# Softmax reciprocals as powers on GpSimd, and the scaling of one attention's probabilities on ScalarE

## The chip, the core and the metric

The kernel runs on one core of one Trainium2 chip. The metric is the device time of one execution in microseconds (us). TensorE (PE in the profile; its weight loads are PEld) multiplies matrices, VectorE (DVE) and ScalarE (ACT) work on columns of up to 128 partitions, GpSimd (POOL) does small work beside them, and SyncE (SP) issues most loads. Each engine runs its own instructions in a fixed order; between engines an instruction waits for semaphores that others raise.

## The reference

A two-layer decoder trunk on 512 tokens of width 1024, in float32. What matters here are its two attentions, both causal, with 8 heads:

```python
# layer 0, differential attention: two softmaxes per head, d = 64
s = einsum('bqhcd,bkhcd->bhcqk', q_blk, k) * d ** -0.5
p = softmax(where(causal, s, -inf))
a = p[:, :, 0] - lam * p[:, :, 1]
o = einsum('bhqk,bkhe->bqhe', a, v)        # then RMSNorm over each head
# layer 1, latent attention: shared keys and values, one softmax per head
s = (einsum(qn, k_nope) + einsum(qr, k_rope)) * (128 + 64) ** -0.5
p = softmax(where(causal, s, -inf))
o = einsum('bhqk,bkhe->bqhe', p, v)
```

Around them stand RMSNorms, the projections, rotary embeddings and a squared-ReLU MLP of width 4096 in each layer.

## The kernel before

**Matrices.** Each float32 operand is split into a high and a low part (`...h`, `...l`) and each product is three matmuls (`mm3`, lines 359 to 361), so TensorE has work nearly all the time. The splits cost VectorE and ScalarE time: ScalarE copies the high part of a weight (line 108), VectorE subtracts it for the low part (line 120).

**The two attention stages.** A task is one head (8) and one block of 128 query rows (4), so there are 32 tasks in the differential attention (`task_a`, names a00 to a73: head, block) and 32 in the latent attention (`task_b`, b00 to b73). Block i looks at n = 128 (i + 1) keys. The tasks are Python generators. A `Weave` steps through the active tasks, and between steps it pulls matmuls of the next heads' projections (`Filler`), so that the tasks' waits lie beside other matmuls. `LAG_A` and `LAG_B` say how many steps a task lets pass before each of its parts. A scheduler then sets the order in which each engine's instructions stand, by what each of them waits for; no order in these stages is written out by hand.

**One task of the differential attention.** TensorE writes two score tiles into PSUM (tile `s`, two banks). VectorE adds the mask and takes the smallest of the negated row (line 531, a pair of instructions for each softmax). ScalarE takes the exponential, with the row sums as a second result (line 533): z0 and z1. Then VectorE works out one column, f = z0 · nlam / z1, in two instructions (lines 585 and 586), and adds p1 · f to p0 (line 587; z0 goes out in the later RMSNorm). In `attend` TensorE transposes the block (tile `tr`, two banks, line 334), ScalarE and VectorE copy its high and low parts (`ath`, `atl`, lines 553 and 554), and after every second block TensorE multiplies with the values (tile `o`, one bank).

**One task of the latent attention.** One score tile, the same mask and exponential with the row sum `tot`, then VectorE takes 1/tot (line 622) and multiplies the whole block by it (line 623), and `attend` follows. The head's result is split from the bank `o` (`onh` on ScalarE, `onl` on VectorE, lines 345 and 346) before the next head may write there.

**GpSimd** has little to do: sums of squares (line 376), powers of -0.5 for the RMSNorms (lines 330 and 606, and at the end `fr`), a scaling near the end.

`small` gives one-column tiles out of a ring of 48. Lines with number 51 in the profile belong to the stretches at the start and the end whose order is kept as the program has it.

Of the kernel before, what the change touches and what calls it, by code (L numbers as in the profile page):

```python
# [10 lines left out]
F32 = mybir.dt.float32  # L11
F32R = mybir.dt.float32r
AF = mybir.ActivationFunctionType
ALU = mybir.AluOpType

P = 128
# [257 lines left out]
def trunk(ctx: ExitStack, tc: tile.TileContext, io: dict, out: bass.AP):  # L274
    nc = Engines(tc)
    PSUM = bass.MemoryType.PSUM

    const = ctx.enter_context(tc.tile_pool(name="const", bufs=1))
# [7 lines left out]
    def big(name, dt=F32):  # L286
        return ap.tile([P, T], dt, name=name, tag="big", bufs=NBIG)

    def small(name, n=8):
        return ap.tile([P, n], F32, name=name, tag="small", bufs=48)  # L290

    def bank(name, tag):
        return ps.tile([P, T], F32, name=name, tag=tag, bufs=BANKS[tag])
# [38 lines left out]
    def transposes(dst, src_of, n=NT):  # L332
        for i in range(n):
            nc.tensor.transpose(dst[:, i * P:(i + 1) * P], src_of(i), ident)

    def row_ps(cols, name):

        dst = bank(name + "_ps", "tr")
        transposes(dst, lambda i: cols[:, i:i + 1].to_broadcast([P, P]))
        return dst  # L340
# [10 lines left out]
    def split(src, name, scale=None, tiles=None):  # L351
        h, l = tiles or (big(name + "h", F32R), big(name + "l", F32R))
        split_into(h, l, src, scale)
        return h, l

    def mm3(dst, a, b, start, stop, **kw):

        (ah, al), (bh, bl) = a, b
        nc.tensor.matmul(dst, ah, bh, start=start, stop=False, **kw)  # L359
        nc.tensor.matmul(dst, ah, bl, start=False, stop=False, **kw)  # L360
        nc.tensor.matmul(dst, al, bh, start=False, stop=stop, **kw)  # L361
        us = 3 * PASS * max(256, dst.shape[-1])
        later.spent(us)
        return us

    def sub(pair, *idx):
        return tuple(t[idx] for t in pair)
# [122 lines left out]
    def mm2(dst, q, k, rest, tok, n, start):  # L490

        nc.tensor.matmul(dst, q[:, tok], k[:, :n], start=start, stop=False)
        nc.tensor.matmul(dst, q[:, tok], rest[:, :n], start=False, stop=True)
        later.spent(2 * PASS * max(256, n))
# [27 lines left out]
    def wait(ticks):  # L522
        for _ in range(ticks):
            yield

    def softmax_parts(s, i, scale, total, name):

        n = P * (i + 1)
        st = small(name + "st", 1)
        sm = big(name + "sm")  # L530
        nc.vector.tensor_tensor_reduce(
            sm[:, :n], s[:, :n], mask[:, T - n:], -scale, 3e38, ALU.add, ALU.min, st)
        nc.scalar.activation(sm[:, :n], sm[:, :n], AF.Exp, bias=st, scale=-1.0, accum_out=total)
        return sm
# [8 lines left out]
    def attend(hd, a, i, lag):  # L543

        name, gq, ii = hd.name, i // 2, i % 2
        if ii == 0:
            hd.a = [ap.tile([P, 4, 2 * P], F32R, name=f"{name}at{n}{gq}", tag=f"at{n}", bufs=2) for n in "hl"]
        ath, atl = hd.a
        tr = bank(f"{name}tr{i}", "tr")
        transposes(tr, lambda j: a[:, j * P:(j + 1) * P], i + 1)  # L550
        cols = (ALL, slice(0, i + 1), slice(ii * P, (ii + 1) * P))
        src = tr[:, :(i + 1) * P].rearrange("p (j q) -> p j q", q=P)
        nc.scalar.copy(ath[cols], src)
        nc.vector.tensor_sub(atl[cols], src, ath[cols].bitcast(F32))
        if ii == 0:
            return
        yield from wait(lag)
        if gq == 0:
            hd.o = bank(name + "o", "o")
        weave.need(lambda: len(hd.quarter.v) == 2)  # L560
        vs = hd.quarter.vs(hd.hh)
        for j in range(i + 1):
            lo = P if j == i else 0
            mm3(hd.o[:, gq * 2 * P + lo:(gq + 1) * 2 * P], vs(j), (ath[:, j, lo:], atl[:, j, lo:]), j == 0, j == i)

    def task_a(hd, i, heads):

        name, n, tok = hd.name, P * (i + 1), slice(i * P, (i + 1) * P)
        qt = hd.quarter
        weave.need(lambda: len(qt.qs) > hd.hh and len(qt.ks) > hd.hh)  # L570
        q, k = qt.qs[hd.hh], qt.ks[hd.hh]
        if i == 0:
            hd.z = small(name + "z", 4)
        z0, z1 = hd.z[:, i:i + 1], small(name + "z1", 1)
        got = []
        for c in range(2):
            s = bank(f"{name}s{i}{c}", "s")
            mm2(s[:, :n], q[c], k[0][c], k[1][c], tok, n, True)
            got.append(softmax_parts(s, i, SCALE_A, (z0, z1)[c], f"{name}{i}{c}"))
        if i == NT - 1:  # L580
            keys_read.add(hd.at)
        yield from wait(LAG_A[1])
        p0, p1 = got
        f = small(name + "f", 1)
        nc.vector.reciprocal(f, z1)
        nc.vector.tensor_scalar(f, f, z0, nlam, op0=ALU.mult, op1=ALU.mult)
        nc.vector.scalar_tensor_tensor(p0[:, :n], p1[:, :n], f, p0[:, :n], op0=ALU.mult, op1=ALU.add)
        yield from wait(LAG_A[2])
        yield from attend(hd, p0, i, LAG_A[3])
        if i < NT - 1:  # L590
            return
        yield from wait(LAG_N[0])
        osb = big(name + "osb")
        nc.scalar.copy(osb, hd.o)
        yield from wait(LAG_N[1])
        otok = bank(name + "otok", "tr")
        transposes(otok, lambda j: osb[:, j * P:(j + 1) * P])
        ss, r = small(name + "ss", 4), small(name + "r", 4)
        junk = big(name + "junk")
        for j in range(NT):  # L600
            cols = slice(j * P, (j + 1) * P)
            nc.scalar.activation(junk[:, cols], otok[:, cols], AF.Square, accum_out=ss[:, j:j + 1])
        e = small(name + "e", 4)
        nc.vector.scalar_tensor_tensor(e, hd.z, SUBLN_EPS, hd.z, op0=ALU.mult, op1=ALU.mult)
        nc.vector.scalar_tensor_tensor(e, ss, 1.0 / P, e, op0=ALU.mult, op1=ALU.add)
        nc.gpsimd.tensor_tensor(r, e, mhalf.to_broadcast([P, 4]), op=ALU.pow)
        yield from wait(LAG_N[2] + LAG_N[3])
        rbo = row_ps(r, name + "rb")
        nc.vector.scalar_tensor_tensor(osb, osb, gsub, rbo, op0=ALU.mult, op1=ALU.mult)
        heads[hd.at] = split(osb, name + "on")  # L610

    def task_b(hd, i, heads):
        name, n, tok = hd.name, P * (i + 1), slice(i * P, (i + 1) * P)
        qt = hd.quarter
        weave.need(lambda: len(qt.qs) > hd.hh and len(qt.ks) > hd.hh and qt.qr and krs)
        s = bank(f"{name}s{i}", "s")
        mm3(s[:, :n], sub(qt.qs[hd.hh], ALL, tok), sub(qt.ks[hd.hh], ALL, slice(0, n)), True, False)
        mm2(s[:, :n], qt.qr[0][hd.hh], *krs[0], tok, n, False)
        tot, rcp = small(name + "tot", 1), small(name + "rc", 1)
        p = softmax_parts(s, i, SCALE_B, tot, f"{name}{i}")  # L620
        yield from wait(LAG_B[1])
        nc.vector.reciprocal(rcp, tot)
        nc.vector.tensor_scalar_mul(p[:, :n], p[:, :n], rcp)
        yield from wait(LAG_B[2])
        yield from attend(hd, p, i, LAG_B[3])
        if i == NT - 1:
            yield from wait(LAG_N[0])
            heads[hd.at] = split(hd.o, name + "on")
# [496 lines left out]
    def late_loads():  # L1125
        nc.sync.dma_start(mask, io["c_mask"])
        for n, name in enumerate(("lambda_q1", "lambda_k1", "lambda_q2", "lambda_k2")):
            nc.sync.dma_start(lam4[:, n, :], io[name].broadcast_to([P, HD]))
    mhalf = const.tile([P, 1], F32, name="mhalf")
    nc.kept = True  # L1130
    nc.vector.memset(mhalf, -0.5)
    ones = const.tile([P, P], F32R, name="ones")
    nc.vector.memset(ones.bitcast(F32), 1.0)
    many = big("many", F32R)
# [74 lines left out]
    for i in range(NT):  # L1209
# [10 lines left out]
    nlam = const.tile([P, 1], F32, name="nlam")  # L1220
# [10 lines left out]


    tasks = [task_a(hd, i, heads_a) for hd in (Head(f"a{h}", h, quarters_a[h // 2], h % 2) for h in range(NH))
             for i in range(NT)]
    fill = Filler(fill_a)
# [71 lines left out]
    def stages(gen, *at):  # L1307
        for us in at:
# [5 lines left out]
    Filler([dq, dkv, krj] + first_b).drain()  # L1314

    tasks = [task_b(hd, i, heads_b) for hd in (Head(f"b{h}", h, quarters_b[h // 2], h % 2) for h in range(NH))
             for i in range(NT)]
    fill = Filler(fill_b)
# [76 lines left out]
```

## Time and profile before

| | us |
|---|---|
| median of 3 runs | 1123.54 (1123.17 to 1124.42) |
| the profiled execution | 1124.63 |
| its span in the trace | 1122.9 |

Of the span TensorE is busy 1106.7 us (99%), VectorE 805.2 (72%), ScalarE 588.8 (52%), GpSimd 61.6 (5%). The differential attention runs from about 50 to 240 us, the latent attention from about 652 to 740 us. A busy share is an average over stages: within the two attentions VectorE is far busier than 72%, which a table of stretches shows. A row of a timeline has its start, its length, the engine, the line, the operation and the tiles (result<-operands); in brackets stands the idle time ahead of it and what ended it.

### The profile page before, as it was taken

What the parts mean: (1) busy time and instruction counts of PE and PEld (TensorE: products, weight loads), DVE (VectorE), ACT (ScalarE), POOL (GpSimd) and SP (SyncE); (2) the same over time, 40 slices, a digit from 0 to 9 for tenths busy, and PEclk for the clock granted to TensorE, in tenths of its full rate; (3) what the DMA queues carried; (4) which work ended last, traced back from release to release, by engine and by line L of the source; (5) the groups of instructions that cost most, each with busy time, mean ns of one, the idle gap of its engine ahead of it and who ended that gap; (6) DMA issues with size and microseconds to landing.
All of it is one profiled execution on the core that took longest, in us unless ns stands there. A gap on an engine that the chain in (4) does not pass through costs nothing. (4 is left out here: it accounts for less than half of the span.)

```text
span 1122.9 us, 14485 instructions
## 1 busy us (share of the span) xinstructions
PE 1106.7 (99%) x5434; PEld 925.3 (82%) x5434; DVE 805.2 (72%) x1417; ACT 588.8 (52%) x1114; POOL 61.6 (5%) x56
## 2 busy tenths in 40 slices
PE   8999999999999999999999999999999999999997
PEld 7889998878888888888887889888888888888885
DVE  6998989964765875886675898855296686687533
ACT  6566666654555455454344666535545445445333
POOL 1000000031000000000022000003000000000011
PEclk8999999999999999999999999999999999999999
DMA  7321221245242142111332211133414315311221
GB/s 230 107 75 57 76 76 58 67 143 155 66 147 97 57 150 94 57 57 40 111 94 90 80 57 38 57 131 94 150 39 150 113 38 161 103 38 57 76 76 75
DMA packets 92517, 102.09 MB, mean 91 GB/s; under 512 B 5104, under 2 KB 74398, under 8 KB 92446
## 3 DMA queue, kind: packets, MB, share of 16 engines
q1 hardware_dynamic: 91166, 99.51, 28.2%
q10 hardware_dynamic: 1280, 1.65, 0.4%
q8 instruction: 43, 0.70, 0.3%
q14 instruction: 28, 0.23, 0.1%
HBM read 99.05 MB, written 2.10 MB: 90 GB/s over the span
## 5 line engine op out<-in xcount | busy, mean ns | idle before, releaser
L359 PE MATMUL m1u<-xn0h,m1u_0h 128*128 128x512 f32 x128 | 50.4, 393 | 0.0
L359 PE MATMUL m1u<-xn1h,m1u_1h 128*128 128x512 f32 x128 | 50.2, 392 | 0.0
L361 PE MATMUL m1u<-xn0h,m1u_0l 128*128 128x512 f32 x128 | 50.0, 390 | 0.0
L360 PE MATMUL m1u<-xn0l,m1u_0h 128*128 128x512 f32 x128 | 50.0, 390 | 0.0
L359 PE MATMUL m0u<-xm0h,m0u_0h 128*128 128x512 f32 x128 | 50.0, 390 | 0.0
L361 PE MATMUL m0u<-xm0h,m0u_0l 128*128 128x512 f32 x128 | 50.0, 390 | 0.0
L361 PE MATMUL m1u<-xn1h,m1u_1l 128*128 128x512 f32 x128 | 49.9, 390 | 0.0
L360 PE MATMUL m1u<-xn1l,m1u_1h 128*128 128x512 f32 x128 | 49.9, 390 | 0.0
L360 PE MATMUL m0u<-xm0l,m0u_0h 128*128 128x512 f32 x128 | 49.9, 390 | 0.0
L361 PE MATMUL m0u<-xm1h,m0u_1l 128*128 128x512 f32 x128 | 49.9, 390 | 0.0
L360 PE MATMUL m0u<-xm1l,m0u_1h 128*128 128x512 f32 x128 | 49.9, 390 | 0.0
L359 PE MATMUL m0u<-xm1h,m0u_1h 128*128 128x512 f32 x128 | 49.8, 389 | 0.0
L120 DVE TENSOR_TENSOR m1u_1l<-m1u_1r,m1u_1h 128x1024 fp32r<-128x1024 f32 x16 | 19.6, 1226 | 32.4 <-ACT m1u_1h L108 32.0
L120 DVE TENSOR_TENSOR m0u_1l<-m0u_1r,m0u_1h 128x1024 fp32r<-128x1024 f32 x16 | 19.9, 1246 | 28.0 <-ACT m0u_1h L108 27.7
L108 ACT CAST m1u_1h<-m1u_1r 128x1024 fp32r<-128x1024 f32 x16 | 16.8, 1052 | 42.5 <-PE m1u L360 29.3
L120 DVE TENSOR_TENSOR m0u_0l<-m0u_0r,m0u_0h 128x1024 fp32r<-128x1024 f32 x16 | 19.9, 1245 | 25.7 <-ACT m0u_0h L108 25.6
L120 DVE TENSOR_TENSOR m1u_0l<-m1u_0r,m1u_0h 128x1024 fp32r<-128x1024 f32 x16 | 19.6, 1224 | 26.0 <-ACT m1u_0h L108 26.0
L108 ACT CAST m0u_1h<-m0u_1r 128x1024 fp32r<-128x1024 f32 x16 | 16.8, 1051 | 40.5 <-PE m0u L360 29.7
L345 ACT CAST krest<-m0A 128x512 fp32r<-128x512 f32 x36 | 22.0, 618 | 27.1 <-PE m0w L360 13.7
L345 ACT CAST krest<-m1A 128x512 fp32r<-128x512 f32 x36 | 22.0, 618 | 26.4 <-PE m1w L360 14.6
L346 DVE TENSOR_TENSOR krest<-m0A,krest 128x512 fp32r<-128x512 f32 x36 | 24.5, 687 | 15.1 <-ACT krest L345 15.1
L346 DVE TENSOR_TENSOR krest<-m1A,krest 128x512 fp32r<-128x512 f32 x36 | 24.4, 687 | 14.0 <-ACT krest L345 14.0
(2905 smaller groups left out, 3719.9 us busy)
## 6 DMA issues: line engine op xcount, KB each, us to landing
m0u_0r<-in_w_up SPq DMA_DIRECT2D x16, 512.0 KB, 3.8
m0u_1r<-in_w_up SPq DMA_DIRECT2D x16, 512.0 KB, 3.7
m1u_0r<-in_w_up SPq DMA_DIRECT2D x16, 512.0 KB, 3.7
m1u_1r<-in_w_up SPq DMA_DIRECT2D x16, 512.0 KB, 4.3
m0B<-in_w_down SPq DMA_DIRECT2D x12, 512.0 KB, 4.3
m0B<-in_w_down SPq DMA_DIRECT2D x24, 256.0 KB, 5.2
m1B<-in_w_down SPq DMA_DIRECT2D x12, 512.0 KB, 3.7
res<-in_w_down SPq DMA_DIRECT2D x12, 512.0 KB, 3.6
```

The source lines that it names most:

```text
L108: self.nc.scalar.copy(d(h), v(self.raws[n]))
L120: eng.tensor_sub(d(to), v(self.raws[n]), d(h).bitcast(F32))
L345: nc.scalar.copy(h, src)
L346: nc.vector.tensor_sub(l, src, h.bitcast(F32))
L359: nc.tensor.matmul(dst, ah, bh, start=start, stop=False, **kw)
L360: nc.tensor.matmul(dst, ah, bl, start=False, stop=False, **kw)
L361: nc.tensor.matmul(dst, al, bh, start=False, stop=stop, **kw)
```

## The change

It touches the reciprocals of both attentions:

```diff
@@ task_a
+        rz1 = small(name + "rz", 1)
+        nc.gpsimd.tensor_tensor(rz1, z1, mone, op=ALU.pow)
         yield from wait(LAG_A[1])
         p0, p1 = got
         f = small(name + "f", 1)
-        nc.vector.reciprocal(f, z1)
-        nc.vector.tensor_scalar(f, f, z0, nlam, op0=ALU.mult, op1=ALU.mult)
+        nc.vector.scalar_tensor_tensor(f, z0, nlam, rz1, op0=ALU.mult, op1=ALU.mult)
         nc.vector.scalar_tensor_tensor(p0[:, :n], p1[:, :n], f, p0[:, :n], op0=ALU.mult, op1=ALU.add)
@@ task_b
         p = softmax_parts(s, i, SCALE_B, tot, f"{name}{i}")
+        nc.gpsimd.tensor_tensor(rcp, tot, mone, op=ALU.pow)
         yield from wait(LAG_B[1])
-        nc.vector.reciprocal(rcp, tot)
-        nc.vector.tensor_scalar_mul(p[:, :n], p[:, :n], rcp)
+        nc.scalar.activation(p[:, :n], p[:, :n], AF.Copy, scale=rcp)
@@ constants
+    mone = const.tile([P, 1], F32, name="mone")
+    nc.vector.memset(mone, -1.0)
```

GpSimd gets 64 powers of one column, each issued right behind its exponentials. VectorE loses a reciprocal in each of the 64 tasks and the scaling in 32; ScalarE gets the 32 scalings. The scheduler also moves other instructions. On TensorE the order of the differential attention stays as it was up to a place in head a7, and in the latent attention some groups of scores and transposes stand a few rows later.

On VectorE, in the differential attention, head a7, block 0 (`a700sm` and `a701sm` are the two probability tiles, `res<-oa` adds an output projection to the residual), the kernel before has

```order
L531 ISA a701sm,a701st<-a7s_2544,mask 128x128
L531 ISA a701st 128x1
L447 TENSOR_TENSOR res<-oa_2552,res 128x512
L585 RECIPROCAL a7f<-a7z_2536 128x1
L586 TENSOR_SCALAR a7f<-a7f,a7z,nlam 128x1
L587 SCALAR_TENSOR_TENSOR a700sm<-a701sm,a7f,a700sm 128x128
```

and the changed kernel, at the same place,

```order
L531 ISA a701sm,a701st<-a7s_2574,mask 128x128
L531 ISA a701st 128x1
L587 SCALAR_TENSOR_TENSOR a7f<-a7z,nlam,a7rz 128x1
L447 TENSOR_TENSOR res<-oa_2584,res 128x512
L588 SCALAR_TENSOR_TENSOR a700sm<-a701sm,a7f,a700sm 128x128
```

Two columns have become one, which now stands right behind the mask of its own softmax, with the addition to the residual behind it.

On ScalarE, in the latent attention's last head and a half (`b5onh` is the high part of head b5's result, `b6ath` and `b7ath` copies of transposed blocks, `b7rc` the reciprocals), the kernel before has

```order
L533 ACTIVATE b71sm,b7tot<-b71sm,b71st 128x256
L345 CAST b5onh<-b5o 128x512
L553 CAST b6ath_7175<-b6tr_7197 128x4x128
L533 ACTIVATE b72sm,b7tot<-b72sm,b72st 128x384
L553 CAST b7ath_7229<-b7tr_7231 128x128
L533 ACTIVATE b73sm,b7tot<-b73sm,b73st 128x512
```

and the changed kernel has

```order
L533 ACTIVATE b70sm,b7tot<-b70sm,b70st 128x128
L624 ACTIVATE b70sm<-b70sm,b7rc 128x128
L553 CAST b6ath_7210<-b6tr_7212 128x3x128
L533 ACTIVATE b71sm,b7tot<-b71sm,b71st 128x256
L345 CAST b5onh<-b5o 128x512
L624 ACTIVATE b71sm<-b71sm,b7rc 128x256
L533 ACTIVATE b72sm,b7tot<-b72sm,b72st 128x384
L553 CAST b6ath_7210<-b6tr_7232 128x4x128
L624 ACTIVATE b72sm<-b72sm,b7rc 128x384
L533 ACTIVATE b73sm,b7tot<-b73sm,b73st 128x512
L553 CAST b7ath_7264<-b7tr_7266 128x128
L624 ACTIVATE b73sm<-b73sm,b7rc 128x512
```

A scaling (line 624) follows each exponential, in the case of b70 with nothing between the two; over the 32 tasks there are eleven such pairs.

## Rows read from the trace of the kernel before

**Rows 1.** Busy time by stretch; columns as the first line says.
```profile
core 0: us, PE busy (x) PEld busy (x) DVE busy (x) ACT busy (x) POOL busy (x), PEclk, DMA share, GB/s
50.00:100.00 50.00, 49.31 (x263) 41.52 (x262) 48.53 (x118) 32.45 (x73) 0.00 (x0) 1.00 0.24 74
100.00:150.00 50.00, 49.62 (x343) 45.73 (x342) 44.36 (x119) 35.65 (x94) 3.40 (x3) 1.00 0.22 65
150.00:222.00 72.00, 71.80 (x437) 62.73 (x435) 66.20 (x173) 48.09 (x130) 3.41 (x3) 1.00 0.21 66
652.00:722.00 70.00, 69.69 (x445) 62.07 (x444) 61.41 (x176) 42.91 (x111) 0.00 (x0) 1.00 0.17 54
```
**Rows 2.** PE's waits in both attentions: us in total, times, longest.
```profile
PE a1tr L334 <- DVE a120sm L587: 0.4, 1, 0.4
PE a1o L360 <- DVE a1atl L554: 0.3, 1, 0.3
...
PE b1o L359 <- DVE b0onl L346: 0.3, 1, 0.3
```
**Rows 3.** What VectorE waited for ahead of line 585: first and last of ten.
```profile
  ACT a521sm L533: 0.9, 1
...
  ACT a711sm L533: 0.2, 1
```
**Rows 4.** Timeline, block a20, from the second mask to the sum p0.
```profile
101.40 0.08 DVE L531 DVE_READ_ACCUMULATOR2_ANT a201st<- 128x1 f32 x1
102.00 0.19 ACT L533 ACTIVATION_READ_ACCUMULATOR a201sm<-a201sm,a201st 128x1 f32 x1
102.22 0.17 DVE L585 RECIPROCAL a2f<-a2z 128x1 f32<-128x1 f32 x1 [0.74 <-ACT a201sm L533]
102.42 0.27 DVE L586 TENSOR_SCALAR a2f<-a2f,a2z,nlam 128x1 f32<-128x1 f32 x1
102.73 0.35 DVE L587 SCALAR_TENSOR_TENSOR a200sm<-a201sm,a2f,a200sm 128x128 f32<-128x128 f32 x1
```
**Rows 5.** Timeline at the end: one-column powers on GpSimd and their neighbours.
```profile
1108.61 0.21 DVE L51 TENSOR_SCALAR fe<-fss 128x1 f32<-128x1 f32 x1 [0.79 <-ACT fjunk L51]
1108.90 0.55 POOL L51 TENSOR_TENSOR fr<-fe,mhalf 128x1 f32<-128x1 f32 x1 [12.56 <-DVE fe L51]
1109.48 0.73 ACT L51 ACTIVATE rt<-rt,fr 128x512 f32<-128x512 f32 x1 [0.91 <-POOL fr L51]
...
1111.55 0.74 DVE L51 SCALAR_TENSOR_TENSOR rt<-rt,fr,gfin 128x512 f32<-128x512 f32 x1
1111.71 0.99 POOL L51 TENSOR_TENSOR fr<-fe,mhalf 128x1 f32<-128x1 f32 x1 [2.26 <-DVE fe L51]
```
**Rows 6.** Timeline: an addition on GpSimd, and VectorE beside it.
```profile
573.68 2.10 POOL L376 TENSOR_TENSOR ssq_b<-ssq_b,sq 128x512 f32<-128x512 f32 x1 [6.28 <-ACT sq L375]
574.55 1.77 DVE L886 TENSOR_TENSOR res<-res,m0t 128x512 f32<-128x512 f32 x1
```
**Rows 7.** One line's instructions: ns least, median, most of eight.
```profile
L886 DVE TENSOR_TENSOR res<-res,m0t x8: 681/694/1780, 558.2 to 597.4; 128x512 f32<-128x512 f32 x8
```
**Rows 8.** Timeline: sums p0 and the transposes that read them, a22 and a73.
```profile
112.42 0.62 DVE L587 SCALAR_TENSOR_TENSOR a220sm<-a221sm,a2f,a220sm 128x384 f32<-128x384 f32 x1
...
116.67 0.38 PE L334 MATMUL a2tr<-ident,a220sm 128*128 128x128 f32 x2
...
223.07 0.75 DVE L587 SCALAR_TENSOR_TENSOR a730sm<-a731sm,a7f,a730sm 128x512 f32<-128x512 f32 x1
...
224.59 0.60 PE L334 MATMUL a7tr<-ident,a730sm 128*128 128x128 f32 x4
```
**Rows 9.** Timeline: head b5's result leaves its bank, head b6 enters.
```profile
730.14 0.57 ACT L345 CAST b5onh<-b5o 128x512 fp32r<-128x512 f32 x1
...
730.91 0.69 DVE L346 TENSOR_TENSOR b5onl<-b5o,b5onh 128x512 fp32r<-128x512 f32 x1
...
731.84 0.28 PE L359 MATMUL b6o<-b6ath,vb3vh 128*128 128x256 f32 x1
```

## The prediction, made before the changed kernel ran

> **What bounds the kernel now.** I read the table of stretches first. TensorE is busy for 49.31 of 50 us, 49.62 of 50 and 71.80 of 72 in the differential attention and for 69.69 of 70 in the latent one, at a granted clock of 1.00 (2.4 GHz) [rows 1]. So a shorter VectorE or ScalarE can give back no more than the little that TensorE waits: of its waits for VectorE in the two attentions the ones listed are 0.4, 0.3 and 0.3 us [rows 2]. Next comes the engine that loses work. VectorE is busy for 48.53 of the first 50 us, and for 44.36 of 50 and 66.20 of 72 after that [rows 1]: it is nearly as full as TensorE. What it waits for there matters more than how full it is. Ahead of the reciprocal (line 585) it stood idle ten times, from 0.9 down to 0.2 us, each time for the exponential of the same block [rows 3]. Such an idle moment is a chain, VectorE's mask, ScalarE's exponential, VectorE's column, in which VectorE's next instruction stands behind the waiting one. That is the place of the change: it makes that chain longer.
>
> **One power on GpSimd.** The cheapest measured case: VectorE's `fe` starts at 1108.61 and takes 0.21, to 1108.82; the power of one column runs from 1108.90 for 0.55; ScalarE's reader starts at 1109.48 [rows 5]. From producer to consumer that is 0.66 us. The next power takes 0.99: it starts at 1111.71, in the middle of a VectorE instruction with two operands in SBUF that ends at 1112.29, and itself ends at 1112.70, 0.41 later [rows 5]. The Trainium skill warns of such spans on GpSimd (Perfetto Trace Analysis, "GPSIMD Engine Instruction"): it calls them unreliable and wants the spacing between instructions instead. Here the two agree, 0.55 of span in 0.66 of spacing, and the sum would be the same by either.
>
> **Differential attention, what goes.** In block a20 the reciprocal starts at 102.22 and the second column at 102.42 [rows 4], so 0.20 us go with the reciprocal. The instruction that stays (0.27) is of the same size. 32 x 0.20 = 6.4 us less on VectorE. Bounds: 0.1 each, since a short instruction costs less where nothing behind it depends on it (3.2), and 0.31, the spacing that the second column has to p0's sum at 102.73 (9.9).
>
> **Differential attention, what comes.** In a20 the sum z1 is ready at 102.19 and the reciprocal starts 0.03 later [rows 4]. Now f starts 0.66 later instead: 0.63 more. In the new order nine of the ten blocks with an idle moment [rows 3] still have nothing, or as little as before, between the mask and f: 9 x 0.63 = 5.7 (the tenth, a43, gets other work ahead of f). Blocks that did not wait before wait now. In a70 the residual's addition has slipped behind f, so that VectorE stands there from the mask to f: 0.71 (101.48 to 102.19 in a20, the same size [rows 4]) + 0.66 = 1.4. In a23, a33, a53 and a72, where one instruction stands between, and a31 and a32, where two or three do, the same reckoning (0.7 to 1.05 to the sum, longer for wider blocks, + 0.66, less 0.6 to 1.8 of work between) gives between 0.2 and 1.1, an estimate of 3.0 together. In the remaining sixteen, other work covers the power. That makes 5.7 + 1.4 + 3.0 = 10.1 us of new idle time against 6.4 saved: +3.7.
>
> **The port.** Where VectorE is not idle, the two engines can meet. An addition on GpSimd that starts at 573.68 lasts until 575.78, and VectorE's `res<-res,m0t`, both operands in SBUF, takes 1.77 us beside it [rows 6] where its median is 0.694 [rows 7]: it stood 1.08 us for GpSimd. For a power of one column no such row exists. The bound from above is 0.41, what the power of [rows 5] still took once VectorE was out of its way; from below it is 0. With sixteen powers beside a busy VectorE that is 0 to 6.6 us. About a half of the differential attention's VectorE instructions have two SBUF operands and about a half of those would start inside a power, so I take a quarter: +1.6.
>
> **How much of it reaches TensorE.** Not all blocks are close. In a22 p0 is done at 113.04 and its transpose starts at 116.67, in a73 p0 is done at 223.82 and its transpose starts at 224.59 [rows 8]. The lead at the end, 0.77, is what is left to swallow. VectorE does not wait for TensorE from 50 to 210 us, so it can't make up what it loses, and TensorE, which has already stood for `a1atl` [rows 2], follows it: 3.7 + 1.6 - 0.8 = +4.5.
>
> **Latent attention.** VectorE loses 32 reciprocals and 32 scalings, and was busy for 61.41 of 70 us; it becomes idle there, which gives TensorE at most the 0.3 of b1o [rows 2]. ScalarE gains 32 scalings. At 512 columns one takes 0.73 [rows 5]; narrower ones less, 0.4 at the least; at 0.55 they are 17.6 us. The eleven that stand directly behind their own exponential wait 0.66 for GpSimd, 7.3 in all. ScalarE had 42.91 of 70 [rows 1], so on average there is room (its waits for TensorE shrink), but not at every place. The tightest that I find is the one bank `o`: b5onh from 730.14, b5onl from 730.91 until 731.60, and b6o's first matmul at 731.84, 0.24 later [rows 9]. In the new order the scalings of b62, b63 and b70 and the two waits that go with them stand ahead of b5onh, about 2.3 us, against about 1 us in which ScalarE waits for transposes now: b5onh comes some 1.2 later, and 1.0 of it reaches TensorE. Bounds: -0.3 (the wait of b1o goes and nothing comes) and +5.5 (half of the eleven waits reach TensorE, 3.7, and two such places, 2).
>
> **Sum.** 4.5 + 1.0 = +5.5 us on the profiled execution, whose span is 1122.9 and whose own time, 1124.63, lies 1.1 above the median of the runs. Nothing outside the two attentions changes, so the difference counts from the median: 1123.5 + 5.5 = 1129.0. What a measurement of this kernel can tell from no change is 0.2%, 2.25 us.
>
> **Rivals.**
> *No change.* The order was made with lags of one or two steps so that waits lie beside matmuls, and a22 shows 3.6 us of room [rows 8]. If the blocks that wait have such room, and VectorE makes its losses good in the 222 to 240 stretch, where it has nothing to do, only the latent attention's 1.0 is left, perhaps with the last 0.5 of the other: 1125.0. Against it: the loss adds up block by block, and the room at the end is 0.77.
> *Faster.* The place is 50 to 100 us, where VectorE is the fullest [rows 1] and where TensorE waits for a120sm. In those eight blocks other work stands between the mask and f, so they lose 8 x 0.20 = 1.6 us on VectorE and wait for nothing. If the later chains find cover after all, TensorE gets back its 0.4 and 0.3 and what the matmuls stand in smaller gaps, and 0.3 in the latent attention: 1.0 to 2.5, 1121.2. It decides if the new waits stay under the lead, that is if the 10.1 is below about 7.
> *The port is the price.* The Trainium skill (SBUF — State Buffer, "Who interferes with whom") says that a VectorE instruction with two SBUF inputs and a GpSimd instruction that reads SBUF exclude each other for the whole instruction, whichever came second waiting. [Rows 6] agree. By it each of the sixteen meetings costs in full. As a mechanism of this kernel: 16 x 0.41 = 6.6 instead of 1.6, +5.0, so 1134.0. Against it: many of the neighbours read PSUM, and such rows show no stretch.
> *ScalarE becomes the bound of the latent attention.* The upper bound there, 5.5 instead of 1.0, gives 1133.5. For it: eleven pairs with nothing between. Against it: 27 idle us of 70.
>
> **Chances.** The forecast 0.45, no change 0.25, faster 0.07, the port 0.13, ScalarE 0.10. Faster by over 0.2%: 0.07. Within 0.2%: 0.25. Slower: 0.45 + 0.13 + 0.10 = 0.68. For the range I go from the no-change case with its own spread (1122.8) to the port's case (1134.0); beyond it lie the faster case and both upper bounds together, under 2 in 10. The likeliest case alone has 1126 to 1132.
>
> **What would show it.** Right: VectorE's waits ahead of f are for GpSimd, not ScalarE, some sixteen of them, about 16 us with the old ones; TensorE's waits from 100 to 240 us grow by about 4, mostly behind `a..sm` and `a..atl`; in the latent attention a wait for b5onl near 732. Wrong in size: f waits in far fewer blocks, since ScalarE's sums come earlier; or powers that take 0.9 and more as a rule; or VectorE instructions with two SBUF operands longer than before beside them. Wrong in kind: TensorE's waits in both attentions as short as they are now.

## The result, and the profile after

The changed kernel takes 1136.02 us (1133.63 to 1137.46, four runs) against 1123.51 of the kernel before: 1.0107 times as long, with an interval of 1.0093 to 1.0121, or 12.0 us (10.4 to 13.6). The prediction was 1129.0 with a range up to 1134.0: the sign is right, the size under half, and the measured time lies above the range. The profiled execution of after took 1134.75, with a span of 1132.7.

**Where the time went.** The same matmuls are looked up in both timelines (start, length, engine, line, operation, tiles): the first transposes of each attention, and the first matmuls of the two MLPs behind them. Before:

```profile
63.71 0.27 PE L334 MATMUL a0tr<-ident,a000sm 128*128 128x128 f32 x1
...
252.62 0.39 PE L359 MATMUL m0u<-xm0h,m0u_0h 128*128 128x512 f32 x1
...
659.01 0.28 PE L334 MATMUL b0tr<-ident,b00sm 128*128 128x128 f32 x1
...
774.28 0.39 PE L359 MATMUL m1u<-xn0h,m1u_0h 128*128 128x512 f32 x1
```

After:

```profile
60.11 0.27 PE L334 MATMUL a0tr<-ident,a000sm 128*128 128x128 f32 x1
...
254.17 0.39 PE L359 MATMUL m0u<-xm0h,m0u_0h 128*128 128x512 f32 x1
...
661.90 0.27 PE L334 MATMUL b0tr<-ident,b00sm 128*128 128x128 f32 x1
...
784.58 0.39 PE L359 MATMUL m1u<-xn0h,m1u_0h 128*128 128x512 f32 x1
```

The shift is -3.60, +1.55, +2.89 and +10.30 us. So the differential attention loses 5.15, the stretch between the attentions 1.34, the latent attention 7.4. The 3.6 us at the start are not the change's: in before's profiled run TensorE's granted clock was 0.65 from 8 to 12 us and 0.50 from 12 to 16, in after's 1.00. Of the profiled runs below, those of experiments 1, 2 and 9 have that stretch too, those of 3, 5 and 14 don't. It hides 3.6 us of the loss in this pair of traces. The 1.34 in the middle go with another such stretch, near 604 us (last section).

**TensorE, by stretch** (answers to [rows 1], same columns). From 652 to 722 us it is busy for 65.08 instead of 69.69:

```profile
100.00:150.00 50.00, 47.66 (x318) 43.17 (x317) 40.93 (x104) 34.74 (x91) 7.27 (x11) 1.00 0.22 63
150.00:222.00 72.00, 70.22 (x416) 61.38 (x415) 61.56 (x155) 45.68 (x123) 11.93 (x16) 0.98 0.19 60
652.00:722.00 70.00, 65.08 (x414) 57.07 (x413) 49.96 (x123) 50.75 (x129) 13.45 (x24) 1.00 0.15 46
```

VectorE has become idle (49.96 where it had 61.41) and TensorE does not gain from it. What TensorE waits for (answers to [rows 2]: us in total, times, longest):

```profile
PE a1o L360 <- DVE a1atl L554: 1.4, 1, 1.4
PE a7s L492 <- ACT k7d L482: 1.2, 2, 0.8
...
PE a3o L360 <- DVE a3atl L554: 0.8, 1, 0.8
PE a7s L493 <- DVE krest L483: 0.5, 1, 0.5
...
PE b1o L359 <- DVE b0onl L346: 1.7, 1, 1.7
PE b1tr L334 <- DVE b1atl L554: 0.9, 1, 0.9
PE b6o L359 <- DVE b5onl L346: 0.9, 1, 0.9
PE b3o L359 <- DVE b2onl L346: 0.8, 1, 0.8
```

In the latent attention these are waits for two PSUM tiles: `o` (behind `onl`) and `tr` (behind `atl`), each of which ScalarE empties first. There are eight of them, 6.0 us in all; before there was one, the 0.3 of `b1o` [rows 2].

**The chain in block a20** (answers to [rows 4]):

```profile
97.84 0.07 DVE L531 DVE_READ_ACCUMULATOR2_ANT a201st<- 128x1 f32 x1
...
98.43 0.18 ACT L533 ACTIVATION_READ_ACCUMULATOR a201sm<-a201sm,a201st 128x1 f32 x1
...
98.76 0.54 POOL L583 TENSOR_TENSOR a2rz<-a2z,mone 128x1 f32<-128x1 f32 x1 [0.39 <-ACT a201sm L533]
...
99.33 0.22 DVE L587 SCALAR_TENSOR_TENSOR a2f<-a2z,nlam,a2rz 128x1 f32<-128x1 f32 x1 [1.42 <-POOL a2rz L583]
```

ScalarE's sum is there at 98.61; f starts 0.72 later, where the forecast had 0.66, and VectorE stands for 1.42 where it stood for 0.74. Over the stage VectorE stands 20 times ahead of f for GpSimd, 17.4 us in all; the first and the last of eight groups (us, times):

```profile
  POOL a2rz L583: 4.4, 4
...
  POOL a0rz L583: 0.4, 1
```

**ScalarE in the latent attention.** The timeline of two blocks, ScalarE alone:

```profile
698.54 0.41 ACT L533 ACTIVATE b40sm<-b40sm,b40st 128x128 f32<-128x128 f32 x1
698.84 0.20 ACT L533 ACTIVATION_READ_ACCUMULATOR b40sm<-b40sm,b40st 128x1 f32 x1
699.76 0.40 ACT L624 ACTIVATE b40sm<-b40sm,b4rc 128x128 f32<-128x128 f32 x1 [0.72 <-POOL b4rc L622]
700.07 0.46 ACT L553 CAST b3ath<-b3tr 128x384 fp32r<-128x384 f32 x1
700.43 0.51 ACT L533 ACTIVATE b41sm<-b41sm,b41st 128x256 f32<-128x256 f32 x1
...
701.75 0.51 ACT L624 ACTIVATE b41sm<-b41sm,b4rc 128x256 f32<-128x256 f32 x1 [0.72 <-POOL b4rc L622]
702.16 0.57 ACT L345 CAST b2onh<-b2o 128x512 fp32r<-128x512 f32 x1
```

Behind each wait stand the copies that free TensorE's banks: `b3ath` and `b2onh`. There are 25 such waits of 0.2 to 0.7, 13.0 us in all: 7.5 at the eleven scalings that stand directly behind their exponential, 5.5 at fourteen of the fifteen with one instruction between; by head, the first and the last of eight (us, times):

```profile
  POOL b4rc L622: 2.8, 4
...
  POOL b0rc L622: 0.8, 2
```

### The profile page after: what moved, and what is told of

It is laid out like the page before. It is cut to its first block, busy times and chain, and to the rows that moved or that the text cites. A ratio compares the mean times of both kernels' runs of the same rounds, so it can differ in the third digit from the quotient of the medians.

```text
span 1132.7 us, 14530 instructions
## 1 busy us (share of the span) xinstructions
PE 1108.8 (98%) x5434; PEld 925.1 (82%) x5434; DVE 789.2 (70%) x1322; ACT 603.3 (53%) x1146; POOL 101.2 (9%) x120
## 5 line engine op out<-in xcount | busy, mean ns | idle before, releaser
L376 POOL TENSOR_TENSOR ssq_b<-ssq_b,sq 128x512 f32<-128x512 f32 x7 | 11.6, 1662 | 324.5 <-ACT sq L375 324.5
```

The lines of the kernel that those rows point to most:

```text
L376: eng(nc).tensor_add(accum, accum, sq)
```

## The experiments

Theory one: an engine that stands in its own order for GpSimd's power is the price, in both attentions. Its rivals: the scaling's own work on ScalarE; the port (VectorE standing for a power beside it, as in the prediction); the mere length of the way from the scores to the transposes. Differences in us are ratios times 1123.5; the numbers in brackets behind a ratio are its 95% interval.

**1. Only the differential attention's edit.** The first half of the diff.

> Only the differential attention's edit is made (power on GpSimd, f from one VectorE instruction); the latent attention is as before. By the forecast's term for this part +4.5 us on 1123.5, and the changed kernel's trace gives +5.0 in that part, of which up to 1.7 is a stretch at half clock near 205 us: 1127 to 1130. If the two parts share their loss in another way (VectorE's delay here is given back before the latent attention and the loss arises there), it is under +2: 1124 to 1125.5. TensorE's waits for f's successors (a1atl, a3atl, a0atl) stay at 2.5 us or more in the first case.

1129.15: 1.0043 (1.0031 to 1.0056), +4.8. The forecast's +4.5 for this part holds, and the waits `a1atl` 1.4, `a3atl` 0.8 and `a0atl` 0.6 are back.

**2. Only the latent attention's edit.** The second half.

> Only the latent attention's edit is made (power on GpSimd, scaling on ScalarE); the differential attention is as before. The forecast's term was +1.0 (1124.5). The trace of the changed kernel puts +7.4 between 652 and 740 us: by that 1129.5 to 1132.5, with TensorE's waits for onl and atl of the latent attention at 5 to 6 us. If the loss there hangs on what the first part left behind (an order of work that comes late), it is nearer 1126.

1131.12: 1.0064 (1.0051 to 1.0077), +7.2. The parts add up to the whole (4.8 + 7.2 against 12.0), and the miss is here: +1.0 was forecast. ScalarE's waits for GpSimd are the same 13.0 us, by the same heads, and TensorE's eight waits the same 6.0.

**3. The reciprocal back on VectorE, right behind the softmax; scaling on ScalarE.** Against experiment 2:

```diff
-        nc.gpsimd.tensor_tensor(rcp, tot, mone, op=ALU.pow)
+        nc.vector.reciprocal(rcp, tot)
         yield from wait(LAG_B[1])
         nc.scalar.activation(p[:, :n], p[:, :n], AF.Copy, scale=rcp)
```

> The scaling is on ScalarE as in the change, but the reciprocal stays on VectorE, issued right behind the softmax; no power on GpSimd; the differential attention is as before. Theory one, ScalarE stands in order for GpSimd's power (13.0 us of such waits): the waits shrink to the 0.2 to 0.3 of a VectorE reciprocal, about 5 us in all, and the loss falls from the 7 of the edit as a whole to +2 to +4 (1125.5 to 1127.5). Theory two, the 17.6 us of scaling on ScalarE are the price, whoever makes the reciprocal: +6 to +7.5 (1129.5 to 1131).

1125.15: 1.0014 (1.0005 to 1.0024), +1.6. Block b40 in the ScalarE timeline, the same order of instructions as after:

```profile
688.20 0.41 ACT L533 ACTIVATE b40sm<-b40sm,b40st 128x128 f32<-128x128 f32 x1
688.50 0.20 ACT L533 ACTIVATION_READ_ACCUMULATOR b40sm<-b40sm,b40st 128x1 f32 x1
688.93 0.40 ACT L623 ACTIVATE b40sm<-b40sm,b4rc 128x128 f32<-128x128 f32 x1 [0.23 <-DVE b4rc L621]
689.80 0.48 ACT L553 CAST b3ath<-b3tr 128x384 fp32r<-128x384 f32 x1 [0.47 <-PE b3tr L334]
```

The wait is 0.23 instead of 0.72, and behind it ScalarE now waits for TensorE. TensorE's listed waits in this attention fall from 6.0 to 1.5 (`b1o` 1.3, `b6tr` 0.2). ScalarE's waits for the column are 3.2 us in 12, a little under the 5 that I expected, and so is the time. With ScalarE's work unchanged, 5.6 of the 7.2 us are gone.

**4. The scaling on ScalarE by a constant.** Against experiment 2:

```diff
-        nc.gpsimd.tensor_tensor(rcp, tot, mone, op=ALU.pow)
         yield from wait(LAG_B[1])
-        nc.scalar.activation(p[:, :n], p[:, :n], AF.Copy, scale=rcp)
+        nc.scalar.activation(p[:, :n], p[:, :n], AF.Copy, scale=0.01)
```

> The scaling of the latent attention's probabilities is on ScalarE as in the change, but by a constant 0.01 in place of the reciprocal of the sum (the normalisation is left out): ScalarE does the same 32 scalings and waits for nobody's column, neither GpSimd nor VectorE; the differential attention is as before. If the wait in ScalarE's order is the price, the work alone costs what the run with VectorE's reciprocal left of it or less: 0 to +1.6 (1123.5 to 1125.5). If the scaling's own work is the price: +5 to +7 (1128.5 to 1131).

1124.26: 1.0005 (0.9994 to 1.0015). The kernel leaves out the normalisation; the same 32 scalings without a wait cost nothing that can be told from none:

```profile
652.00:722.00 70.00, 69.11 (x446) 61.86 (x445) 53.21 (x128) 51.49 (x136) 0.00 (x0) 1.00 0.17 54
```

ScalarE is busier than after the change (51.49 against 50.75) and TensorE has 69.11 instead of 65.08. The work on ScalarE is not the price.

**5. The power on GpSimd, the scaling on VectorE.** Against the kernel before:

```diff
+        nc.gpsimd.tensor_tensor(rcp, tot, mone, op=ALU.pow)
         yield from wait(LAG_B[1])
-        nc.vector.reciprocal(rcp, tot)
         nc.vector.tensor_scalar_mul(p[:, :n], p[:, :n], rcp)
```

> The power is on GpSimd, the scaling stays on VectorE; the differential attention is as before. Theory one in its strict form (any engine that waits in order for the power loses) expects VectorE to stand for it instead of ScalarE, but VectorE has more room here: 0 to +3 (1123.5 to 1126.5). Theory two (the scaling on ScalarE) expects no loss: -0.5 to +0.5 (1123 to 1124). A loss of +5 or more would say that the power on GpSimd is the cost wherever its reader is.

1127.15: 1.0033 (1.0020 to 1.0046), +3.7, a little over the expected 3. VectorE now stands for the power, 9.8 us in 14 waits, though it does less than before. So in this attention the power costs with either reader, about half as much with VectorE, which stands 14 times where ScalarE stood 25 times. VectorE did not have more room, as the expectation has it: from 652 to 722 us it is busy for 56.80 of 70 here, ScalarE for 50.75 after the change.

**6. The differential attention's edit, f one step later.** Experiment 1 with

```diff
-LAG_A = (2, 1, 2, 2)
+LAG_A = (2, 2, 2, 2)
```

> The differential attention's edit alone, with one step more between the power and f (LAG_A's second number 2 for 1). Theory one, the in-order wait for the power is the price (17.4 us of waits ahead of f in the changed kernel): the waits go almost entirely (under 4 us left), VectorE keeps the 6.4 us that it saves, and the time is that of the kernel before or less: 1121.5 to 1124.5. Rival, the length of the chain from the scores to the transposes is the price, whether an engine waits in it or not: a step more makes it longer, 1129 to 1133 (the edit alone was 1129.15).

1123.27: 0.9993 (0.9983 to 1.0004). Of the 17.4 us ahead of f one wait is left:

```profile
  POOL a7rz L583: 0.5, 1
```

The longer way costs nothing here; with the waits gone, the loss is gone. No faster than the kernel before by this measure.

**7. Control: the kernel before with the later step alone.** The same line, no power.

> The kernel before with LAG_A's second number 2 for 1 and nothing else: the control for the run with the power and the later f (1123.27). If the later step alone gains (VectorE's idle moments ahead of the reciprocal go too, 5 us of them): 1121.5 to 1123.5, and the power adds nothing. If the longer way costs and the 6.4 us saved on VectorE made it good there: 1125 to 1129.

1124.56: 1.0004 (0.9994 to 1.0015). It falls between the two expectations: the later step by itself neither gains nor costs, and what VectorE saves (in experiment 6 its one-column instructions for f take 6.7 us, here 13.5) shows in no time that can be told from no change.

**8. The latent attention's edit, the scaling one step later.** Experiment 2 with LAG_B's second number 2 for 1.

> The latent attention's edit alone, with one step more between the power and the scaling (LAG_B's second number 2 for 1). Theory one, ScalarE's wait in order for the power is the price (13.0 us of waits): they fall under 3 us and what is left is what the scaling's own work costs, +1.6 as with the reciprocal on VectorE: 1124 to 1126.5. Rival, the length of the chain from the scores to the transposes and the one bank o behind it: a step more makes it longer, 1131 to 1136 (the edit alone was 1131.12).

1130.82: 1.0056 (1.0042 to 1.0071). The time lies just under the rival's range, but the waits did not go: 12.4 us for GpSimd are left. In only four of 32 blocks another exponential came between a block's own and its scaling (one in experiment 2). The run does not separate the theories.

**9. The longer way alone, in the latent attention.** The kernel before with LAG_B's second number 2 for 1.

> The kernel before with LAG_B's second number 2 for 1 and nothing else: reciprocal and scaling of the latent attention stay on VectorE and come a step later, so the way from the scores to the transposes is longer and nobody waits for GpSimd. If the length of the way is the price: +3 to +7 (1127 to 1131). If the wait in order is: 0 to +1.5 (1123.5 to 1125).

1126.60: 1.0023 (1.0013 to 1.0033), +2.6, between the two. TensorE waits 1.8 us ahead of `b5o`, `b3o`, `b1o` and `b2o`. So a longer way from the scores to the one bank `o` has a price of its own in this attention, unlike in the other. The edit also moves other work: here the mask of b63 stands ahead of `b4onl` on VectorE, before it stood behind it. How much of the 2.6 is the length alone is not shown.

**10. Powers read by a copy on ScalarE.** Beside the unchanged code:

```diff
+        nc.gpsimd.tensor_tensor(rcu, tot, mone, op=ALU.pow)
...
+        nc.scalar.copy(rcv, rcu)
```

> The kernel before with 32 powers on GpSimd in the latent attention, each read by a one-column copy on ScalarE at the place of the change's scaling, whose result nobody reads; reciprocal and scaling stay on VectorE. ScalarE gets the wait and hardly any work (about 0.2 us a copy). If the wait in order is the price: about 10 us of ScalarE's waits for GpSimd and +3 to +6 (1126.5 to 1129.5). If it is the scaling's work or the longer way of the probabilities themselves (which here don't wait for the power): 0 to +1.5 (1123.5 to 1125).

1123.42: 0.9996 (0.9987 to 1.0005). The scheduler put the copies where the powers were done: 0.2 us of waits, not ten. So it says nothing of the wait; it shows that 32 powers and 32 tiny copies cost nothing.

**11. 64 powers that nobody reads.** The kernel before, with the change's powers beside the reciprocals.

> The kernel before with the change's 64 powers on GpSimd added at the places that the change gives them; nothing reads their results, so nobody can wait for them. The port theory: VectorE instructions with two operands in SBUF stand for a power of one column, 0.1 to 0.41 for each of 64: with the half of them that fall beside such instructions +3 to +13 (1126.5 to 1136). Theory one: the power alone costs nothing, it waits itself: -0.5 to +1 (1123 to 1124.5).

1125.53: 1.0009 (0.9999 to 1.0019), +1.0. The time lies between the expectations, the difference at theory one's upper end and under the port's +3; the interval just holds no change. None of VectorE's instructions beside a power is more than 0.08 longer than its like in before. Two meetings with VectorE instructions that have both operands in SBUF, GpSimd first, then VectorE:

```profile
74.39 1.75 POOL L583 TENSOR_TENSOR a0rz<-a0z,mone 128x1 f32<-128x1 f32 x1 [5.72 <-ACT a031sm L533]
...
95.42 0.54 POOL L583 TENSOR_TENSOR a1rz<-a1z,mone 128x1 f32<-128x1 f32 x1 [6.47 <-ACT a131sm L533]
```

```profile
73.88 0.68 DVE L507 TENSOR_TENSOR q4t<-q4t,q4sw 128x512 f32<-128x512 f32 x1
74.48 1.25 DVE L120 TENSOR_TENSOR wk_0l<-wk_0r,wk_0h 128x1024 fp32r<-128x1024 f32 x1
...
95.62 0.67 DVE L507 TENSOR_TENSOR q3t<-q3t,q3sw 128x512 f32<-128x512 f32 x1
```

At 74.39 the power begins while VectorE is at `q4t`; the next instruction of the kind follows without a gap, both take their usual lengths, and the power lasts 1.75, to 76.14, 0.41 after the second one's end. So it is the power that stands, not VectorE. At 95.62 VectorE's instruction begins inside a power, and both have their usual lengths side by side.

**12. The changed kernel with each power made twice.**

```diff
+        nc.gpsimd.tensor_tensor(small(name + "rx", 1), z1, mone, op=ALU.pow)
         nc.gpsimd.tensor_tensor(rz1, z1, mone, op=ALU.pow)
```

and the same for `tot`.

> The changed kernel with each power made twice, one after the other, so that the reader's power ends about 0.55 us later. Theory one: the 20 waits ahead of f grow by 0.55 each (11 us), which TensorE follows nearly one to one as VectorE is the fullest there, and the 14 of ScalarE by as much (7.7), of which about a half reaches TensorE as of the first 13.0: +13 to +18 over the changed kernel, 1149 to 1154. If the waits had room behind them and the cost lay elsewhere (order of work, scaling), under +4: below 1140.

1162.82: 1.0342 (1.0328 to 1.0357), +38.4, above every expectation. ScalarE's waits grow from 13.0 to 28.3 us, VectorE's ahead of f from 17.4 to 25.7. The same marks as above give a loss of 16.4 in the differential attention (5.15 after) and 23.3 in the latent one (7.4): 11 and 16 more. From mark to mark of the latent attention, after and here (columns as in [rows 1]):

```profile
661.90:784.60 122.70, 116.33 (x678) 99.94 (x677) 79.34 (x166) 78.26 (x182) 24.87 (x36) 1.00 0.22 69
```

```profile
676.60:815.20 138.60, 123.12 (x678) 105.50 (x677) 79.28 (x166) 78.93 (x182) 40.76 (x66) 0.95 0.19 62
```

TensorE is idle for 15.5 us here and for 6.4 after, 9.1 more for 15.3 more of ScalarE's waits; the other 7 are longer busy time, at a mean clock of 0.95. In the differential attention TensorE's idle time grows by 8.1, from 5.7 to 13.8, for 8.3 more of VectorE's waits, and its busy time by 3.

**13. Both attentions, with the latent reciprocal on VectorE.** The expectation speaks of f one step later; the kernel that ran had LAG_A as before, so it is experiments 1 and 3 together.

> The whole change with both waits taken out as far as the runs showed how: in the differential attention the power on GpSimd and f one step later, in the latent attention the reciprocal on VectorE right behind the softmax and the scaling on ScalarE. If the parts add up (-0.7 and +1.6 against before): 1123.5 to 1126, far from the change's 1136. If the two stages disturb one another: above 1127.

1129.15: 1.0046 (1.0033 to 1.0058), +5.2, against 4.8 + 1.6 of its parts. The parts add up; the text's own question waits for the next run.

**14. The same with f one step later**, experiments 6 and 3 together.

> The whole change with both waits taken out: in the differential attention the power on GpSimd and f one step later (LAG_A's second number 2), in the latent attention the reciprocal on VectorE right behind the softmax and the scaling on ScalarE. If the parts add up (-0.7 and +1.6 against before): 1123.5 to 1126, against the change's 1136. If the two stages disturb one another: above 1127.

1124.26: 1.0003 (0.9992 to 1.0013). The change with both waits cut short costs nothing, and gains nothing:

```profile
652.00:722.00 70.00, 68.73 (x437) 60.80 (x435) 54.25 (x151) 54.59 (x139) 0.00 (x0) 1.00 0.16 54
```

VectorE is idle for 15.75 of 70 us in the latent attention, where it was for 8.59 [rows 1], and TensorE is no fuller. No version was found that beats the kernel before.

## Why the prediction was wrong

**One power.** Nearly right: 0.66 forecast from sum to reader, 0.72 measured in a20 (98.61 to 99.33) and in b40 (699.04 to 699.76).

**Differential attention.** Right in its sum, in part by luck. About 16 us of waits ahead of f in sixteen blocks were forecast, 17.4 us in 20 came; TensorE was to wait about 4 longer, mostly behind `atl`, and its listed waits from 50 to 240 us grow from 1.8 to 5.5, with 2.8 of the 5.5 behind `atl`; +4.5 was forecast, +4.8 (3.5 to 6.3) measured. Experiments 6 and 7 show the cause: with the waits gone, so is the loss. Two terms do not bear it out. The port's +1.6 is not there: no VectorE instruction was longer. And a term that I did not have stands in its place in the profiled run of after, TensorE's clock near 205 us (below), 1.7 us by its rows.

**Latent attention.** This is the step that failed: "about 2.3 us, against about 1 us in which ScalarE waits for transposes now: b5onh comes some 1.2 later, and 1.0 of it reaches TensorE". That place behaves as forecast: `b6o` waits 0.9 for `b5onl`. But I took the tightest place for the only one, and let ScalarE's mean of 27 idle us in 70 cover the others; TensorE waits at eight places, 6.0 us. Experiment 2 gives +7.2 (5.7 to 8.7) for the term, over its upper bound of 5.5 (whose own parts, 3.7 and 2, make 5.7). Two reasons are in the rows. The waits are 13.0 us, not 7.3: the eleven scalings directly behind their exponential came as forecast, 7.5, but of the fifteen with one instruction between fourteen wait too, 5.5 us, since an instruction of 0.3 to 0.6 covers only a part of 0.7. And TensorE, busy for 69.69 of 70, had no slack of its own: what delays `ath` or `onh` is passed on in good part, 6.1 us of idle time for the first 13.0 of waiting and 9.1 for the 15.3 that experiment 12 added. The scaling, which I counted as ScalarE's load, was sized right (17.6 us forecast, 18.0 measured) and is worth nothing: with it and without a wait the time is that of before (experiment 4).

**What stays open.** In the latent attention the power both holds up ScalarE's order and lengthens the way of the probabilities. Experiment 9 prices a longer way without a power at +2.6, another lengthening than the power's 0.7 a block; the run that was to keep the way long and take the wait away (8) kept the wait. So the power with its waits is shown to be the cost of most of the 7.2: about 5.6 by experiment 3, 6.6 by experiment 4, each give or take some 2 us. How that splits between standing in order and a longer way is not shown.

**The rivals.** "ScalarE becomes the bound" gave 1133.5 and had the right attention and the right kind of price, waits that reach TensorE, but too small; ScalarE did not become the bound (50.75 of 70 us). "The port is the price" failed: see experiment 11. The page named there (the Trainium skill, SBUF — State Buffer, "Who interferes with whom") has the second comer wait, whichever it is. [Rows 6] agreed for an addition of 512 columns. For a power of one column the rows agree where the power comes second (74.39 in experiment 11); where VectorE does (95.62) it was no longer than usual, so the term had the price on the wrong engine. Above 1134.0 the prediction saw only both upper bounds together; the port's came to nothing, and the latent attention's was passed.

**No change, faster.** Both rested on room behind the waits. Experiment 6 shows that there is room for a later step in the differential attention, not for an engine that stands: the difference between the two is what the no-change case missed. Nor is VectorE free from 222 to 240 us, where that case has it make its losses good: before, it is busy there for 10.48 of 18.

## What to carry to other kernels

Here, moving a short operation to an idle engine lengthened the chain of whoever reads it, and the reader's engine paid by standing, with everything that was queued behind it. So price the added wait at every place where it stands in the order, also behind one short instruction, rather than by the engine's mean idle share, and ask what of the queue frees a bank for the bound engine. Where the reader could be put behind other work of its engine, as in the differential attention, the same hop cost nothing, and with the bound engine full it gained nothing either; in the latent attention a later step did not get the reader behind other work (experiment 8).

## What the runs showed of the hardware

TensorE's granted clock fell to half (0.50, 1.2 GHz, from 206 to 208 us) after a short stretch of waiting. In the profiled run of after (columns as in [rows 1]), 3 us with TensorE busy for 1.83 come ahead of a stretch with a mean of 0.57:

```profile
202.00:205.00 3.00, 1.83 (x12) 1.21 (x10) 2.53 (x4) 2.92 (x8) 1.71 (x1) 1.00 0.00 0
205.00:209.00 4.00, 3.49 (x9) 2.77 (x10) 3.07 (x10) 2.25 (x13) 0.84 (x1) 0.57 0.49 133
```

Before, TensorE was busy for 2.89 there and kept its clock:

```profile
202.00:205.00 3.00, 2.89 (x21) 2.29 (x19) 2.96 (x7) 2.37 (x6) 0.00 (x0) 1.00 0.00 0
205.00:209.00 4.00, 3.90 (x19) 2.77 (x19) 3.53 (x12) 3.09 (x14) 0.73 (x1) 1.00 0.43 131
```

So 1.7 us of waits for `k7d` and `krest` were followed by about as much again in clock (0.43 of 4 us). It is no certain price: in experiment 13 TensorE waited the same 1.2 and 0.5 us there and kept a clock of 1.00:

```profile
203.00:206.00 3.00, 1.89 (x13) 1.27 (x11) 2.56 (x6) 2.93 (x8) 1.71 (x1) 1.00 0.00 0
206.00:209.00 3.00, 2.43 (x11) 1.96 (x12) 2.94 (x10) 1.52 (x10) 0.00 (x0) 1.00 0.51 175
```

Another such stretch, near 604 us, is in the profiled runs of after and of experiments 1, 10, 11 and 13 and not in those of before and experiments 2, 3, 4 and 6; what decides it is not shown.

Powers of one column on GpSimd took 0.54 to 0.56 us in 52 of 64 cases of after. The other twelve took up to 1.75: each began during a VectorE instruction with two operands in SBUF and ended 0.39 to 0.42 us after it, or after the next of the kind where that followed without a gap. No VectorE instruction beside a power was more than 0.08 us longer than its like in before, here or in experiment 11.
